# Five late projection chunks, output projection by input quarters, and the first gate through GpSimd's queue

## The chip, the cores and the metric

The kernel runs on one core of one Trainium2 chip. The metric is the device time of one execution in microseconds; the time before is the median of three runs. A profile of one further execution is read beside it. Five engines work side by side: TensorE (PE in the profile, PEld for its weight loads), VectorE (DVE), ScalarE (ACT), GpSimd (POOL) and SyncE (SP), which here only issues DMAs. Each engine runs its own instructions in order. DMAs are issued from the queues of SP, ACT and POOL, and a DMA that has to wait holds up what is behind it on its queue.

## The reference, cut to what matters

One encoder layer on x of 256 rows by 2048 columns, float32, with a conditioning vector c:

```python
mod = silu(c) @ mod_w + mod_b                  # 2048 x 12288
sh_m, sc_m, g_m, sh_f, sc_f, g_f = split(mod, 6)
h = x * (1 + sc_m) + sh_m
q, k, v = split(h @ w_qkv + b_qkv, [2048, 2560])   # 32 query heads, 8 key/value heads of 64
q, k = rope(q), rope(k)
o = softmax over keys with |q - k| <= 128, and a sink logit per head
y = o @ w_o + b_o                              # 2048 x 2048
x = layer_norm(2 ** 0.25 * x + (1 + g_m) * y)
h = x * (1 + sc_f) + sh_f
y = square(relu(h @ w1 + b1)) @ w2 + b2        # 2048 x 8192 x 2048
x = layer_norm(2 ** 0.25 * x + (1 + g_f) * y)
```

Every one of these weights is used once for 256 rows. Some 290 MB come from HBM in one execution.

## The kernel before, in words

**Products.** A float32 product is made of three matmuls in the rounded type float32r: each operand is split in a high and a low part, and `mm3` (L561) adds high x high (L562), high x low (L563) and low x high (L564) in PSUM.

**The weight stream.** All weights come as chunks of 1 MB (128 x 2048) in one written order, `S.q`, planned at L485 to L553. SP loads them into raw buffers (L236): eight at first (`raws` and `raws2`), five from attention step 1 on (`S.deep = False`). A projection chunk is made into two half chunks, each copied to its high part by ScalarE (`wh`, L281) and subtracted to its low part by VectorE (`wl`, L252); up to five halves of each stand ready. A modulation chunk is used straight from its raw buffer: a row chunk by TensorE (`Mod.step`, L336), a column chunk by VectorE (`Col.step`, L376, a multiply and reduce against the spread condition `cb`). `S.pump` advances the stream whenever a half chunk is done.

**Group by group.** The 2048 inputs of the first projection are taken in six groups of 128-wide k tiles (`MIXG`, 1, 1, 2, 4, 4, 4). Once the modulation of a group is there (`columns`, L405), `modulated(g)` makes h of that group: ScalarE the high part (L591), VectorE the full value and the low part (L592, L593). The chunk (g, c) is the part of the projection from group g to the output block c of 512 columns; block order `CORD` counts 4 = keys, 5 = values, 0 to 3 = queries. Each chunk is 24 matmuls of 128 x 512 and ends in `evict`, which adds the two PSUM banks to the accumulator in SBUF (L609), unless `CARRY` says that the next chunk of the same block goes on in the same banks. `ORDER` gives the chunks of each group that run before attention, and the modulation of group g + 1 is planned between the chunks of group g. `modulated(g + 1)` stands in the program in the middle of the last chunk of group g that `ORDER` names.

**Attention steps.** 16 steps of attention are interleaved with chunks that are left: step n takes one chunk. Each has `scores(n)` (L755, L762, exponentials L772), `normalise` (L784), the transposes of the step before (`probs_T`, L794, L796), and every second step `values` (L810, then L813 and L814, which split the result in high and low, `oT[j]`, one j for four steps). `LATE` lists the projection chunks that run in the first steps, `OUT_AT` is the step at which the output projection starts, and `SLOT_FILL` how many chunks of the remaining modulation (the first gate `m_gm` with 16, then that of the feed-forward) are planned in each step. Before, LATE has eight chunks and there are 24 steps, the last eight without scores.

**Output projection.** `project(p, c)` (L852) takes two quarters j of the attention's output at a time: two chunks into the same two PSUM banks, 48 matmuls, then VectorE evicts (p = 0: L890 into `ys` with the output bias; p = 1: L893 to L896, with the gate, the residual and the statistics). The last one, c = 3, keeps the rows apart: all matmuls of row tile 0, then of row tile 1, and `add_gated` (L816, L819 to L821) and the normalisation (`norm_scalars`, `normed`) directly behind each. `project_0(3)` (L899) applies the gate to what `ys` holds for c = 3 ahead of that.

**The first gate.** `m_gm.spread` (L450) transposes the gate to one row, writes that to DRAM (`rowm`, L458) and reads it back into all 128 partitions by two broadcasts (L460), all from ScalarE's queue, at the end of step 15. The buffers are two of the pool `gen` (`g4`).

**What sets the order.** The program is written out in the order above; a scheduler then orders each engine's instructions by what it takes for their readiness. The instructions of `modulated` are kept at their place in program order. Buffers come from pools: `gen` has 20 of 4 KB a partition, `gen2` (`g4b`) six, `psa` five PSUM banks.

Of the kernel before, what the change touches and what calls it, by code (L numbers as in the profile page):

```python
# [11 lines left out]
F32 = mybir.dt.float32  # L12
# [8 lines left out]
S = 256  # L21
NT = S // 128
NK = D // 128
# [5 lines left out]
LN_EPS = 1e-5  # L29
NEG = -1.0e30  # L30
BLK = 4
OUT_AT = 8
X_AT = 16
SLOT_FILL = (2, 1, 2, 1, 2, 1, 2, 1, 1, 2, 1, 2, 1, 2, 1, 2, 2, 2, 1, 2, 1, 2, 0, 0)
MIXG = (1, 1, 2, 4, 4, 4)
MIXP = (1, 1, 1, 2, 2, 2)
FFG = (4, 4, 4, 4)
# [34 lines left out]
def hybrid_kernel(ctx: ExitStack, tc: tile.TileContext, a, out: bass.AP):  # L72
    nc = tc.nc
    cst = ctx.enter_context(tc.tile_pool(name="cst", bufs=1))
    sml = ctx.enter_context(tc.tile_pool(name="sml", bufs=4))
# [238 lines left out]
    S = Stream()  # L314
# [4 lines left out]
    class Mod:  # L319
# [24 lines left out]
        def step(self, raw):  # L344
            w, kc, i = self.w, self.kc, self.i
            if i == 0:
                self.ps = psm.tile([128, 512], F32, name="pm")
            r = raw.rearrange("p (k j n) -> p k j n", k=kc // 2 if self.pairs else kc, j=4)
            self.i += 1
            last = self.i == self.n  # L350
            for k in range(kc):
                kt = i * kc + k
                if self.pairs:
                    if k % 2 == 0:
                        cols = [cact[:, kt + j // 2:kt + j // 2 + 1].to_broadcast([128, 32]) for j in range(4)]
# [67 lines left out]
    class Gate(Group):  # L423
# [26 lines left out]
        def spread(self, g):  # L450

            d, b = self.col[:, 8 * self.p:], self.gb[:, 8 * self.p:]
            nc.vector.tensor_tensor(d, d, b, op=OP.add)
            pt = pst.tile([128, 512], F32, name="pt")
            nc.tensor.matmul(pt[:NK, :128], self.col, ident, start=True, stop=True)
            r = sml.tile([NK, 128], F32, name="grow", bufs=1)
            nc.scalar.copy(r, pt[:NK, :128])
            nc.scalar.dma_start(self.row.rearrange("o (k n) -> (o k) n", k=NK), r)  # L458
            for h in range(2):
                nc.scalar.dma_start(g[h], self.row[:, h * 1024:h * 1024 + 1024].partition_broadcast(128))  # L460
            return lambda c: g[c // 2][:, (c % 2) * 512:(c % 2) * 512 + 512]

    def groups(which, sizes, prods, mb, dst):
# [11 lines left out]
    m_gf = Gate("f", 0, gateb[:, 1])  # L475

    G = len(MIXG)
    LATE = [(4, 3), (5, 3), (3, 4), (4, 4), (5, 4), (3, 5), (4, 5), (5, 5)]

    ORDER = {2: (1, 2, 0), 3: (0, 3, 2, 1), 4: (1, 2, 0), 5: (0, 1, 2)}  # L480
    CARRY = {((1, 2), 2), ((2, 0), 0), ((3, 1), 1), ((4, 0), 0)}
    CARRY |= {(x, x[1]) for x, y in zip(LATE, LATE[1:]) if x[1] == y[1]}
    qk_order = [(g, c) for g in range(2, G) for c in ORDER[g]]
    wq = lambda g, c: S.plan(a["wqkv"][m_mix[g].k0 * 6 // 4 + c])
# [10 lines left out]
    for g in range(2, G):  # L495
        n = len(ORDER[g])
        if g + 1 < G:
            S.side[len(S.q)] = lambda g=g: load_x(g)
        for x, c in enumerate(ORDER[g][1:], 1):
            if g + 1 < G:  # L500
                m_mix[g + 1].plan({2: [0, 0, 3], 3: [0, 3, 2, 2], 4: [0, 4, 4]}[g][x])
            wq(g, c)
        if g == 2:
            m_mix[3].plan(4)
        if g + 1 < G:
            if g == 3:
                m_mix[4].plan(1)
            wq(g + 1, ORDER[g + 1][0])
        if g == 2:
            m_mix[3].plan(1)  # L510
# [7 lines left out]
            if lp[0] < len(late):  # L518
                late[lp[0]].plan()

    OUTS = [(p, c, j) for p in range(2) for c in range(4) for j in (2 * p, 2 * p + 1)]
    for n in range(OUT_AT + 16):
        plan_late(SLOT_FILL[n])
        if n == X_AT:
            S.side[len(S.q)] = lambda: load_rows()
        if n < len(LATE):
            wq(*LATE[n])
        elif n >= OUT_AT and n - OUT_AT < len(OUTS):
            p, c, j = OUTS[n - OUT_AT]
            S.plan(a["wo"][c, j])  # L530
    S.stop = len(S.q)
    plan_late(4)
    W1_FILL = [1, 1, 1, 0, 0, 2, 0, 3, 0, 0, 0, 0, 0, 0, 0, 0]
# [27 lines left out]
    def mm3(ps, xh, xl, wh, wl, start, stop):  # L561
        nc.tensor.matmul(ps, xh, wh, start=start, stop=False)  # L562
        nc.tensor.matmul(ps, xh, wl, start=False, stop=False)  # L563
        S.prev = nc.tensor.matmul(ps, xl, wh, start=False, stop=stop).ins  # L564
# [284 lines left out]
        else:  # L849
            nc.vector.tensor_scalar(z, z, mv[:, 0:1], rstd, op0=OP.subtract, op1=OP.mult)  # L850

    def project(p, c):  # L852

        pss = [psa.tile([128, 512], F32, name="pa") for _ in range(NT)]
        last = p == 1 and c == 3
        ws = [S.main(), S.main()] if last else []
        for x in range(2):
            wh, wl = ws[x] if last else S.main()
            oh, ol = oT[2 * p + x]
            for r2 in (0, 2):  # L860
                for t in range(NT):
                    if last:
                        break
                    for r in (r2, r2 + 1):
                        s = slice(t * 512 + r * 128, t * 512 + r * 128 + 128)
                        mm3(pss[t], oh[:, s], ol[:, s], wh(r), wl(r), x + r == 0, x == 1 and r == 3)
                if not last:
                    S.done()
                    if r2 == 0 or x == 0:
                        yield  # L870
        if last:
            for t in range(NT):
                for x in range(2):
                    oh, ol = oT[2 * p + x]
                    wh, wl = ws[x]
                    for r in range(4):
                        s = slice(t * 512 + r * 128, t * 512 + r * 128 + 128)
                        mm3(pss[t], oh[:, s], ol[:, s], wh(r), wl(r), x + r == 0, x == 1 and r == 3)
                if t == 0:
                    yield  # L880
                add_gated(pss[t], t, c, g1, st)
                sc.append(norm_scalars(st[t]))
                normed(0, t)
            for _ in range(4):
                S.done(False)
            return
        for t, ps in enumerate(pss):
            y = part(ys, t, c)
            if p == 0:
                nc.vector.tensor_add(y, ps, bo(c))  # L890
            else:
                z = part(xs, t, c)
                nc.vector.tensor_add(y, y, ps)  # L893
                nc.vector.tensor_mul(y, y, g1(c))
                nc.vector.scalar_tensor_tensor(z, z, ALPHA, y, op0=OP.mult, op1=OP.add)
                nc.vector.bn_stats(st[t][:, c], z)  # L896
# [25 lines left out]
    S.behind = True  # L922
    for n in range(OUT_AT + 16):
        j, i = n // 4, n % 4
        if n < 16:
            scores(n)
        for f in todo:
            f()
        todo = []
        if n == 1:  # L930
            S.deep = False
        if n < OUT_AT:
            w = qkv(*LATE[n])
        else:
            if n == OUT_AT:
                assert all(h is raws for h in S.home[S.at:]), "an early buffer is still in use"
                ys, bo = [g4b() for _ in range(4)], bias_all(a["bo"], [g4b(), g4b()])
            if n % 2 == OUT_AT % 2:
                w = project(*divmod((n - OUT_AT) // 2, 4))
        mid = mids(n)  # L940
        if j < 3:
            if i == 2:
                turn = rope(j + 1, 1)
                mid += [lambda: next(turn), lambda: next(turn)]
            if i == 3:
                mid.append(lambda: qA.__setitem__(j + 1, next(turn)))
                mid.append(lambda: qT.__setitem__(j + 1, heads_T(qA[j + 1])))
        next(w, None)
        for f in mid:
            f()  # L950
        next(w, None)
        if 0 < n <= 16 and n % 2 == 0:
            todo.append(values(n - 1))
        if n == 15:
            g1 = m_gm.spread([g4(), g4()])
        if n == 16:
            warm = sml.tile([128, 1], F32, name="warm")
            nc.scalar.activation(warm, eps, AF.Sqrt)
            st = [sml.tile([128, 4, 6], F32, name=f"st{t}", bufs=2) for t in range(NT)]
        if n == 18:  # L960
            project_0(3)


# [291 lines left out]
```

## Time and profile before

| | before |
|---|---|
| median of three runs | 1125.22 us (1124.86 to 1127.91) |
| profiled execution | 1127.18 us |
| its span, first to last instruction | 1125.4 us |
| mean granted TensorE clock | 0.978 |
| busy: PE, DVE, ACT, POOL | 1067.9, 786.5, 526.9, 17.1 us |
| moved by DMA | 292.74 MB, 260 GB/s over the span |

The stages lie in the span as follows: groups 0 to 5 up to some 160 us, steps with scores from 163.69 us, the last output projection ends near 379 us, and the feed-forward part runs from 390 us to the end. In the rows, "[9.10 <-DVE g L814]" is the idle time of the engine before the instruction, and what ended it. PE busy is counted with modelled ends of its matmuls, so that one of 128 x 512 counts some 0.39 us, though the next starts after 0.23. A row of a stretch gives busy time and number of instructions for each engine, the granted clock, the DMA engines' busy share and GB/s.

### The profile page before, as it was taken

What the parts mean: (1) busy time and instruction counts of PE and PEld (TensorE: products, weight loads), DVE (VectorE), ACT (ScalarE), POOL (GpSimd) and SP (SyncE); (2) the same over time, 40 slices, a digit from 0 to 9 for tenths busy, and PEclk for the clock granted to TensorE, in tenths of its full rate; (3) what the DMA queues carried; (4) which work ended last, traced back from release to release, by engine and by line L of the source; (5) the groups of instructions that cost most, each with busy time, mean ns of one, the idle gap of its engine ahead of it and who ended that gap; (6) DMA issues with size and microseconds to landing.
All of it is one profiled execution on the core that took longest, in us unless ns stands there. A gap on an engine that the chain in (4) does not pass through costs nothing.

```text
span 1125.4 us, 16314 instructions
## 1 busy us (share of the span) xinstructions
PE 1067.9 (95%) x6554; PEld 883.0 (78%) x6554; DVE 786.5 (70%) x1135; ACT 526.9 (47%) x811; POOL 17.1 (2%) x34
## 2 busy tenths in 40 slices
PE   7687999999979899999999999999999999999995
PEld 6565777677757699998888888888888888888884
DVE  3786898778648966765668787865665656665576
ACT  5422447778643454653345444334444334444340
POOL 1000000000000000000000001000000000000001
PEclk9997999999998899999999999999999999999998
DMA  9999987777984888555678788776555555557521
GB/s 385 425 425 415 413 303 279 278 260 280 367 326 151 321 341 343 192 186 188 198 288 297 263 283 274 294 291 217 185 188 191 202 192 187 187 188 262 187 75 75
DMA packets 43651, 292.74 MB, mean 260 GB/s; under 512 B 4876, under 2 KB 5036, under 8 KB 9784
## 3 DMA queue, kind: packets, MB, share of 16 engines
q1 hardware_dynamic: 40400, 281.96, 67.5%
q0 software_dynamic: 1792, 6.29, 1.8%
q10 hardware_dynamic: 1384, 3.45, 0.8%
q8 instruction: 51, 0.84, 0.3%
q14 instruction: 24, 0.20, 0.0%
HBM read 289.57 MB, written 2.11 MB: 259 GB/s over the span
## 4 chain that ended last, share of the span: by engine, by line
PE 77%; DVE 9%; DMA 7%; ACT 4%; issue 2%; POOL 0%; DVEq 0%; ACTq 0%; POOLq 0%
PE pa L1081 16%; PE pa L564 14%; PE pa L562 14%; PE pa L563 14%; PE pa L1082 8%; DMA raw<-in_mod 5%; PE pa L1058 3%; PE pa L1059 3%; PE pa L1057 3%; DVE raw L376 2%; DVE wl L252 2%; PE pm L336 2%; DMA raw<-in_wqkv 1%; ACT wh L281 1%; ACT g L772 1%
## 5 line engine op out<-in xcount | busy, mean ns | idle before, releaser
L252 DVE TENSOR_TENSOR wl<-raw,wh 128x1024 fp32r<-128x1024 f32 x332 | 403.7, 1223 | 237.9 <-ACT wh L281 236.7
L281 ACT CAST wh<-raw 128x1024 fp32r<-128x1024 f32 x332 | 347.8, 1051 | 439.7 <-PE pa L564 258.7
L564 PE MATMUL pa<-wh,g 128*128 128x512 f32 x816 | 320.7, 394 | 14.0 <-DVE g L814 9.1
L562 PE MATMUL pa<-wh,g 128*128 128x512 f32 x816 | 325.2, 399 | 3.6 <-ACT g L591 2.2
L563 PE MATMUL pa<-wl,g 128*128 128x512 f32 x816 | 321.3, 394 | 0.0
L1081 PE MATMUL pa<-g,wh 128*128 128x512 f32 x768 | 271.6, 399 | 0.0
L1082 PE MATMUL pa<-g,wl 128*128 128x256 f32 x768 | 215.7, 281 | 0.0
L564 PEld LDWEIGHTS pa<-wh,g 128*128 128x128 f32 x816 | 154.6, 189 | 49.3 <-DVE g L814 10.0
L562 PEld LDWEIGHTS pa<-wh,g 128*128 128x128 f32 x816 | 154.9, 190 | 43.5 <-issue 7.1
L563 PEld LDWEIGHTS pa<-wl,g 128*128 128x128 f32 x816 | 155.0, 190 | 31.6 <-DVE wl L252 0.7
L1081 PEld LDWEIGHTS pa<-g,wh 128*128 128x128 f32 x768 | 144.3, 188 | 36.2 <-issue 0.2
L1082 PEld LDWEIGHTS pa<-g,wl 128*128 128x128 f32 x768 | 145.1, 189 | 0.1
L376 DVE CUSTOM_DVE_ANT_0 raw<-raw,cb 128x2048 f32<-128x2048 f32 x54 | 123.5, 2287 | 19.1 <-DMA raw<-in_mod 19.1
L1058 PE MATMUL pa<-g,wh 128*128 128x256 f32 x256 | 73.5, 288 | 2.0 <-DVE g L1001 2.0
L1057 PE MATMUL pa<-g,wh 128*128 128x256 f32 x256 | 73.2, 288 | 0.0
L1059 PE MATMUL pa<-g,wl 128*128 128x256 f32 x256 | 73.0, 286 | 0.0
L336 PE MATMUL pm<-raw,cact 128*32 128x128 f32 (+1 forms) x1216 | 46.6, 292 | 13.7 <-DMA raw<-in_mod 13.3
L336 PEld LDWEIGHTS pm<-raw,cact 128*32 128x32 f32 x1216 | 32.0, 111 | 28.1 <-DMA raw<-in_mod 14.5
L1058 PEld LDWEIGHTS pa<-g,wh 128*128 128x128 f32 x256 | 49.7, 194 | 2.8 <-DVE g L1001 2.3
L1057 PEld LDWEIGHTS pa<-g,wh 128*128 128x128 f32 x256 | 49.8, 195 | 0.4 <-ACT g L993 0.4
L1059 PEld LDWEIGHTS pa<-g,wl 128*128 128x128 f32 x256 | 49.8, 194 | 0.2 <-issue 0.2
L772 ACT ACTIVATE g<-g,nm 128x256 f32<-128x256 f32 x64 | 31.8, 498 | 23.4 <-DVE nm L762 23.3
(171 smaller groups left out, 673.8 us busy)
## 6 DMA issues: line engine op xcount, KB each, us to landing
raw<-in_mod SPq DMA_DIRECT2D x96, 1024.0 KB, 7.4
raw<-in_w SPq DMA_DIRECT2D x64, 1024.0 KB, 4.9
raw<-in_w1b SPq DMA_DIRECT2D x48, 1024.0 KB, 5.0
raw<-in_wqkv SPq DMA_DIRECT2D x24, 1024.0 KB, 10.7
raw<-in_wo SPq DMA_DIRECT2D x16, 1024.0 KB, 7.4
raw<-in_w1a SPq DMA_DIRECT2D x16, 1024.0 KB, 7.0
g<-in_x SPq DMA_DIRECT2D x4, 512.0 KB, 12.1
gb<-in_lnrow POOLq DMA_DIRECT2D x8, 256.0 KB, 6.1
```

What stands on the lines that cost most here:

```text
L252: self.pinned(nc.vector.tensor_sub(l, r, f32(self.hs[n])))
L281: self.pinned(nc.scalar.copy(h, s))
L336: i = nc.tensor.matmul(self.ps[32 * j:32 * j + 32, :w], lhsT[j] if type(lhsT) is list else lhsT, rhs[j], start=self.first, stop=stop)
L376: S.pinned(nc.vector.tensor_tensor_reduce(out=raw, in0=raw, in1=cb, scale=1.0, scalar=0.0, op0=OP.mult, op1=OP.add, accum_out=self.dst))
L562: nc.tensor.matmul(ps, xh, wh, start=start, stop=False)
L563: nc.tensor.matmul(ps, xh, wl, start=False, stop=False)
L564: S.prev = nc.tensor.matmul(ps, xl, wh, start=False, stop=stop).ins
L1057: nc.tensor.matmul(o, wh(w, 128), hh, start=new, stop=False)
L1058: nc.tensor.matmul(o, wh(w, 128), hl, start=False, stop=False)
L1059: nc.tensor.matmul(o, wl(w, 128), hh, start=False, stop=end)
L1081: nc.tensor.matmul(ps, wh(k, 128), hb, start=k == 0, stop=False)
L1082: nc.tensor.matmul(ps[:, :256], wl(k, 128), hb[:, :256], start=False, stop=k == NK - 1)
```

## The change

Three things, in one edit.

The chunks (3,5), (3,4) and (4,3) of the first projection leave `LATE` and are planned in `ORDER`, ahead of attention; the modulation chunks of the following groups are distributed anew between them. `LATE` has five chunks left, and there are 21 steps.

The output projection starts at step 5 instead of 8 and takes one quarter j at a time: first all four c of quarter 0, then of quarter 1, and so on; each `project` is one chunk with 24 matmuls and an eviction of its own. Quarter 0 brings the bias in, quarters 1 and 2 only add, quarter 3 adds, gates and takes the statistics. `SLOT_FILL` fills two modulation chunks into each of the first eight steps, so that the first gate's 16 chunks end with step 7's slot.

The first gate is spread at the end of step 12 instead of 15, by the same three DMAs on GpSimd's queue, into two buffers of `gen2`. `project_0(3)` follows at the end of step 16 instead of 18. The rows of x for the residual (`load_rows`) are loaded at stream position 79 instead of 89.

```diff
-OUT_AT = 8
-X_AT = 16
-SLOT_FILL = (2, 1, 2, 1, 2, 1, 2, 1, 1, 2, 1, 2, 1, 2, 1, 2, 2, 2, 1, 2, 1, 2, 0, 0)
+OUT_AT = 5
+X_AT = 10
+SLOT_FILL = (2, 2, 2, 2, 2, 2, 2, 2, 1, 1, 1, 1, 1, 2, 2, 2, 2, 2, 2, 1, 0)
...
-            nc.scalar.dma_start(self.row.rearrange("o (k n) -> (o k) n", k=NK), r)
+            nc.gpsimd.dma_start(self.row.rearrange("o (k n) -> (o k) n", k=NK), r)
             for h in range(2):
-                nc.scalar.dma_start(g[h], self.row[:, h * 1024:h * 1024 + 1024].partition_broadcast(128))
+                nc.gpsimd.dma_start(g[h], self.row[:, h * 1024:h * 1024 + 1024].partition_broadcast(128))
...
-    LATE = [(4, 3), (5, 3), (3, 4), (4, 4), (5, 4), (3, 5), (4, 5), (5, 5)]
-    ORDER = {2: (1, 2, 0), 3: (0, 3, 2, 1), 4: (1, 2, 0), 5: (0, 1, 2)}
-    CARRY = {((1, 2), 2), ((2, 0), 0), ((3, 1), 1), ((4, 0), 0)}
+    LATE = [(5, 3), (4, 4), (5, 4), (4, 5), (5, 5)]
+    ORDER = {2: (1, 0, 2), 3: (5, 4, 3, 0, 2, 1), 4: (1, 2, 3, 0), 5: (0, 1, 2)}
+    CARRY = {((1, 2), 2), ((2, 2), 5), ((3, 1), 1), ((4, 0), 0)}
...
-                m_mix[g + 1].plan({2: [0, 0, 3], 3: [0, 3, 2, 2], 4: [0, 4, 4]}[g][x])
+                m_mix[g + 1].plan({2: [0, 0, 3], 3: [0, 2, 2, 2, 1, 1], 4: [0, 3, 3, 2]}[g][x])
...
-            if g == 3:
-                m_mix[4].plan(1)
...
-    OUTS = [(p, c, j) for p in range(2) for c in range(4) for j in (2 * p, 2 * p + 1)]
+    OUTS = [(c, js, x) for js in ((0,), (1,), (2,), (3,)) for c in range(4) for x in range(len(js))]
...
-    def project(p, c):
+    def project(js, c):
...
+        for x in range(len(js)):
+            ws.append(S.main())
+            for r in (0, 2):
+                for t in range(NT):
+                    step(x, t, (r, r + 1))
+                S.done()
+                if r == 0 or x < end:
+                    yield
         for t, ps in enumerate(pss):
             y = part(ys, t, c)
-            if p == 0:
+            if n == 0:
                 nc.vector.tensor_add(y, ps, bo(c))
-            else:
+                continue
+            nc.vector.tensor_add(y, y, ps)
+            if n == 3:
                 z = part(xs, t, c)
-                nc.vector.tensor_add(y, y, ps)
                 nc.vector.tensor_mul(y, y, g1(c))
...
-            if n % 2 == OUT_AT % 2:
-                w = project(*divmod((n - OUT_AT) // 2, 4))
+            c, js, x = OUTS[n - OUT_AT]
+            if x == 0:
+                w = project(js, c)
...
-        if n == 15:
-            g1 = m_gm.spread([g4(), g4()])
+        if n == 12:
+            g1 = m_gm.spread([g4b(), g4b()])
+            st = [sml.tile([128, 4, 6], F32, name=f"st{t}", bufs=2) for t in range(NT)]
         if n == 16:
             warm = sml.tile([128, 1], F32, name="warm")
             nc.scalar.activation(warm, eps, AF.Sqrt)
-            st = [sml.tile([128, 4, 6], F32, name=f"st{t}", bufs=2) for t in range(NT)]
-        if n == 18:
             project_0(3)
```

More of the change, by code (lines that the diff above doesn't have):

```diff
@@ L527, in hybrid_kernel @@
             wq(*LATE[n])
-        elif n >= OUT_AT and n - OUT_AT < len(OUTS):
-            p, c, j = OUTS[n - OUT_AT]
-            S.plan(a["wo"][c, j])
+        else:
+            c, js, x = OUTS[n - OUT_AT]
+            S.plan(a["wo"][c, js[x]])
     S.stop = len(S.q)
@@ L850, in normed, with step @@
             nc.vector.tensor_scalar(z, z, mv[:, 0:1], rstd, op0=OP.subtract, op1=OP.mult)
-    def project(p, c):
+    def project(js, c):
         pss = [psa.tile([128, 512], F32, name="pa") for _ in range(NT)]
[L855 to L870, printed above, removed]
+        end, n = len(js) - 1, js[-1]
+        last = n == 3 and c == 3
+        ws = [S.main() for _ in js] if last else []
+        def step(x, t, rs):
+            wh, wl = ws[x]
+            oh, ol = oT[js[x]]
+            for r in rs:
+                s = slice(t * 512 + r * 128, t * 512 + r * 128 + 128)
+                mm3(pss[t], oh[:, s], ol[:, s], wh(r), wl(r), x + r == 0, x == end and r == 3)
         if last:
             for t in range(NT):
[L873 to L878, printed above, removed]
+                for x in range(len(js)):
+                    step(x, t, range(4))
                 if t == 0:
@@ L883, in project @@
                 normed(0, t)
-            for _ in range(4):
+            for _ in range(2 * len(js)):
                 S.done(False)
             return
+        for x in range(len(js)):
+            ws.append(S.main())
[5 more added lines that the diff above has]
+                    yield
         for t, ps in enumerate(pss):
             y = part(ys, t, c)
-            if p == 0:
+            if n == 0:
                 nc.vector.tensor_add(y, ps, bo(c))
-            else:
+                continue
+            nc.vector.tensor_add(y, y, ps)
+            if n == 3:
                 z = part(xs, t, c)
-                nc.vector.tensor_add(y, y, ps)
                 nc.vector.tensor_mul(y, y, g1(c))
@@ L937, in hybrid_kernel @@
                 ys, bo = [g4b() for _ in range(4)], bias_all(a["bo"], [g4b(), g4b()])
-            if n % 2 == OUT_AT % 2:
-                w = project(*divmod((n - OUT_AT) // 2, 4))
+            c, js, x = OUTS[n - OUT_AT]
+            if x == 0:
+                w = project(js, c)
         mid = mids(n)
```

## The prediction

> **What bounds the kernel now.** I began with the page: engine totals and the forty slices.
>
> ```profile
> span 1125.4 us, 16314 instructions
> PE 1067.9 (95%) x6554; PEld 883.0 (78%) x6554; DVE 786.5 (70%) x1135; ACT 526.9 (47%) x811; POOL 17.1 (2%) x34
> ...
> PE   7687999999979899999999999999999999999995
> ...
> PEclk9997999999998899999999999999999999999998
> DMA  9999987777984888555678788776555555557521
> ```
>
> TensorE is busy 95% of the span, and the change neither adds nor removes a matmul. So it can only gain where TensorE stands idle or runs at a lowered clock, and lose by making new such places. Two slices stick out below 400 us: the fourth (PEclk 7), while the DMA row is full, and the thirteenth and fourteenth (PEclk 8). The busy time by stretches and TensorE's waits name them:
>
> ```profile
> 78.00:100.00 22.00, 9.71 (x101) 6.72 (x94) 15.12 (x22) 3.28 (x6) 0.00 (x0) 0.61 1.01 427
> 100.00:320.00 220.00, 217.50 (x1507) 161.01 (x1506) 180.48 (x348) 142.22 (x319) 2.19 (x4) 1.00 0.83 315
> 340.00:346.00 6.00, 6.00 (x15) 4.71 (x16) 3.63 (x5) 1.04 (x1) 0.00 (x0) 0.51 0.16 22
> 392.00:1125.00 733.00, 720.48 (x3990) 621.52 (x3989) 487.74 (x600) 323.85 (x407) 9.86 (x14) 0.99 0.63 223
> ...
> PE pm L336 <- DMA raw<-in_mod: 13.3, 4, 6.5
> PE pa L564 <- DVE g L814: 9.1, 1, 9.1
> ```
>
> Columns are the stretch, its length, then PE, PEld, DVE, ACT and POOL busy, the granted clock, the DMA share and GB/s. From 100 to 320 us and from 392 us on TensorE is the bound: 217.50 of 220 and 720.48 of 733. What can be won lies at 78 to 100 us and around 330 us.
>
> **The gate's stall goes.** The timeline there:
>
> ```profile
> 321.03 0.32 ACTq L458 DMA_DIRECT2D rowm<-grow  x1
> 326.06 0.86 ACTq L460 DMA_DIRECT2D g<-rowm  x2
> 326.96 1.07 ACT L796 COPY g<-pt 128x512 f32<-128x512 f32 x2 [4.52 <-DMA rowm<-grow]
> 327.60 1.14 PE L810 MATMUL pa<-g,g 128*64 128x256 f32 x8 [0.87 <-ACT g L796]
> 337.40 0.69 DVE L903 TENSOR_TENSOR g4b<-g4b,g 128x512 f32<-128x512 f32 x1 [11.28 <-DMA g<-rowm]
> 339.14 0.69 DVE L814 TENSOR_TENSOR g<-pa,g 128x512 fp32r<-128x512 f32 x1
> 339.88 0.79 PE L564 MATMUL pa<-wh,g 128*128 128x512 f32 x1 [9.10 <-DVE g L814]
> ```
>
> ScalarE sends the gate row to DRAM at 321.03 and stands 4.52 us until it has landed, because the broadcast behind it on its queue reads it back. VectorE then stands 11.28 us at `project_0` (L903), which wants the broadcast, and a weight subtraction and the values' subtraction (L814) are queued behind it; TensorE wants those. Cost: 9.10 + 0.87 idle, and then 6 us (340 to 346) at a clock of 0.51, that is 6 x 0.49 = 3.0. Sum 13.0 us.
>
> [...]
>
> After, the spread is issued at the end of step 12 and first read at the end of step 16. Moved with it: VectorE's bias add, two matmuls, a ScalarE copy and three DMAs, all small. The three DMAs pass from ScalarE's queue to GpSimd's, which has nothing behind them but the second bias's load, not wanted before the feed-forward outputs. GpSimd's own wait is for one DMA, and nobody else queues there. The pitch of a step:
>
> ```profile
> 163.69 1.14 PE L755 MATMUL pa<-g,g 64*128 64x256 f32 x8
> 308.76 0.92 PE L755 MATMUL pa<-g,g 64*128 64x256 f32 x6
> ...
> g4b<-in_bo POOLq DMA_DIRECT2D x2, 512.0 KB, 4.5
> ...
> 180.00:200.00 20.00, 19.32 (x131) 13.56 (x128) 18.08 (x39) 13.48 (x35) 1.23 (x2) 1.00 0.66 233
> ```
>
> Scores of steps 0 and 15 lie 145.1 us apart: 9.67 us a step, so the lead is 4 x 9.67 = 38.7 us against 337.40 - 321.03 = 16.4 for row and broadcast as they are. Slack 22.3. A GpSimd-queue broadcast of the same size takes 4.5 us to land, in a stretch where VectorE is busy 18.08 of 20. Term: -13.0 (0 if the cover failed). The new buffers `g4b` are the output bias's, last read in step 8; no wait.
>
> **The third group may start sooner.** TensorE ends group 2 just before 77.57 us and starts group 3 at 90 to 95.65:
>
> ```profile
> 74.90 0.16 DVE L421 TENSOR_TENSOR modm<-pt,pack 128x4 f32<-128x4 f32 x1 [1.34 <-PE pt L419]
> 77.57 1.08 PE L336 MATMUL pm<-raw,cact 128*32 128x128 f32 x32
> 80.02 1.08 PE L336 MATMUL pm<-raw,cact 128*32 128x128 f32 x32 [1.37 <-DMA raw<-in_mod]
> 81.98 2.29 DVE L376 CUSTOM_DVE_ANT_0 raw<-raw,cb 128x2048 f32<-128x2048 f32 x1
> 87.55 1.94 PE L336 MATMUL pm<-raw,cact 128*32 128x128 f32 x32 [6.45 <-DMA raw<-in_mod]
> 89.77 2.07 ACT L591 ACTIVATE g<-g,modm 128x256 fp32r<-128x256 f32 x4
> 92.51 2.29 DVE L376 CUSTOM_DVE_ANT_0 raw<-raw,cb 128x2048 f32<-128x2048 f32 x1 [1.90 <-DMA raw<-in_mod]
> 94.72 0.41 DVE L592 TENSOR_SCALAR g<-g,modm 128x256 f32<-128x256 f32 x1
> 95.17 0.43 DVE L593 TENSOR_TENSOR g<-g,g 128x256 fp32r<-128x256 f32 x1
> 95.65 0.79 PE L564 MATMUL pa<-wh,g 128*128 128x512 f32 x1 [4.00 <-DVE g L593]
> ```
>
> Group 3's own modulation was complete at 75 us; its activation (L591, 89.77) and subtraction (L593) run only behind group 4's modulation weights: the last row chunk (TensorE, 87.55) and the last column chunk (VectorE, 92.51), both waiting for DMA. Numbering the weight stream from 0, these are chunks 31 and 33. In program order the modulation follows chunk 28 (the row at 80.02); after the change it follows chunk 27 (the column at 81.98), and group 4's last row and column move to 32 and 34. Which order the scheduler now writes I can't read off the trace. Best: the subtraction follows the column at 81.98: 81.98 + 2.29 + 0.41 + 0.43 = 85.1 instead of 95.17 + 0.43 = 95.6, -10.5. Worst: it still follows the last column, one 1 MB chunk later at 427 GB/s, +2.5. I take -7, nearer the best, because the program now reaches it before chunk 28 and two more projection chunks lie between it and group 4's last row.
>
> The three chunks that come forward, (3,5), (3,4), (4,3), bring 3 x 2.5 = 7.4 us of DMA into the full stretch, but 3 x 5.46 = 16.4 us of matmuls too (24 a chunk, 0.227 us apart: below, six in 1.36), so groups 4 and 5 arrive behind more work than before. Term 0; 7.4 if that cover were gone.
>
> **What is added.** An output projection by quarters leaves PSUM four times, not two.
>
> ```profile
> 349.62 0.39 PE L564 MATMUL pa<-wh,g 128*128 128x512 f32 x1
> 350.98 0.39 PE L564 MATMUL pa<-wh,g 128*128 128x512 f32 x1
> ...
> L890 DVE TENSOR_TENSOR g4b<-pa,g4b x8: 662/688/692, 258.9 to 318.6; 128x512 f32<-128x512 f32 x8
> ...
> L562 PEld LDWEIGHTS pa<-wh,g 128*128 128x128 f32 x121 | 22.7, 188 | 9.4 <-issue 4.7 <-DVE g4b L890 0.7 <-DVE g L609 0.3
> ```
>
> Out: 14 adds become 30. Projection: 38 become 44, as (3,4), (3,5) and (4,3) no longer hand their banks on. 22 adds x 0.69 = 15 us of VectorE, spread over 270 us in which it has 20% free (180.48 of 220). On the path: in 160 to 310 us TensorE's weight loads waited 0.7 us for L890 in three evictions, 0.23 each; 8 more evictions cost 1.9, I take 2 (0 to 5). The eight gate columns now fall in steps 0 to 4 and before, where VectorE was busy 18.08 of 20: 1 (0 to 5). The four row loads of `x` on SP's queue move some five steps forward; about two steps of weights stand loaded ahead of them (five buffers), and 2 MB at 427 GB/s are 4.9 us: 0, or 4.9 if nothing covered them.
>
> **The tail.** Steps 17 to 23 become 17 to 20.
>
> ```profile
> 367.97 1.28 DVE L893 TENSOR_TENSOR g4b<-g4b,pa 128x512 f32<-128x512 f32 x2
> 373.90 2.29 DVE L376 CUSTOM_DVE_ANT_0 raw<-raw,cb 128x2048 f32<-128x2048 f32 x1
> 376.11 0.69 DVE L819 TENSOR_TENSOR tmp<-pa,g 128x512 f32<-128x512 f32 x1
> 379.29 0.69 DVE L819 TENSOR_TENSOR tmp<-pa,g 128x512 f32<-128x512 f32 x1 [0.55 <-PE pa L564]
> ```
>
> After the last but one column's matmuls VectorE takes 376.11 - 367.97 = 8.1 us until the first half's gating (L819), 3.2 more to the second's. Before, 48 matmuls (10.9 us) ran meanwhile, and the second L819 waited for TensorE. After, 24 run (5.46 us), so it comes 11.3 - 5.9 = 5 us behind TensorE; without the column chunk in between some 2. I take +3 (1.7 to 5).
>
> **Sum.** -13 - 7 + 2 + 1 + 3 = -14. The profiled execution took 1127.18 us (1125.4 span, 1.8 around it), so 1113.2; it lies 2.0 above the median of the runs, 1125.22, so I predict 1111.2, say 1111. Best: -13 - 10.5 + 1.7 = -22, 1103. What a measurement can tell from no change is 0.3%, 3.4 us.
>
> **Rivals.**
>
> Group 3 stays behind the whole of group 4: +2.5 in place of -7, sum -4.5, 1120.7. For it: the order was so in the trace, though the program put chunk 28 last. Against: the program's point moved up.
>
> [...]
>
> Slower: the banks. Every step now takes two fresh PSUM banks of five and must evict them before the next step's projection. If each eviction stood behind a column chunk, 2.3 + 1.3 us less the 1.1 of scores between, 2.5 us a step in the 12 steps 5 to 16 would be 30: -13 - 7 + 30 + 1 + 3 = +14, 1139. It decides from -13 - 7 + 1 + 3 + 12w = +3.4, w = 1.6 us a step. Against it stand the 0.23 us that an eviction cost in the trace.
>
> **Numbers.** Forecast 0.60 (nearly all faster), group 3 behind 0.21 (two thirds of it faster), late gate 0.07 (mostly same), banks or a new stall of that size 0.12 (slower). So faster 0.75, same 0.13, slower 0.12. The likeliest case alone spans 1103 to 1118; the range 1102 to 1124 takes in the next two.
>
> **What would show it.** The 9.10 us wait for L814 and VectorE's 11.28 at `project_0` are gone, and the clock is 1.00 all through the attention steps: the gate. The first group-3 matmul lies at 84 to 90 us, with L591 ahead of group 4's last row: the early part. Evictions to `g4b` without TensorE gaps: the banks. The feed-forward stretch keeps its 733 us. I am wrong if a wait on a row of `in_mod` beyond 6 us stays before group 3, if TensorE idles at each step, or if the last normalisation starts over 5 us after the last projection.

## The result and the profile after

The changed kernel took 1121.55 us (median of 7 runs, 1116.23 to 1123.08), the kernel before 1126.6 beside it: ratio 0.9943, 95% interval 0.9922 to 0.9965. It is faster, by about 5 us between the medians (6.4 between the means of the same runs) and not by the 14 forecast. The 1121.55 us lie inside the stated range, next to the 1120.7 given for group 3 staying behind; as the profile shows, group 3 did not stay behind, so that nearness is chance. The same instruction streams ran a second time as `pin_sqrt` below: 0.9933 (0.9920 to 0.9945). Where several runs are compared, ratios to the kernel before stand, times 1127 us: the change brought 6.4 to 7.6 us.

The profiled execution took 1123.08 us, the longest of the seven. Its page, engine totals and slices:

```profile
span 1121.3 us, 16337 instructions
...
PE 1071.7 (96%) x6554; PEld 884.6 (79%) x6554; DVE 799.9 (71%) x1157; ACT 526.8 (47%) x811; POOL 20.3 (2%) x40
...
PEclk9999999998999799999999999999999999999998
```

The dips of before in slices 4 and 13 are gone from the clock row; slice 14 is deeper (7, before 8), and slice 10 is new. Busy time by stretches (stretch, length, PE, PEld, DVE, ACT, POOL, clock, DMA share, GB/s):

```profile
78.00:100.00 22.00, 20.89 (x172) 16.07 (x171) 17.74 (x25) 4.87 (x7) 0.00 (x0) 1.00 1.01 426
100.00:320.00 220.00, 211.45 (x1460) 155.45 (x1462) 187.51 (x349) 133.86 (x295) 2.81 (x5) 0.98 0.84 322
370.00:392.00 22.00, 11.37 (x110) 9.15 (x113) 17.92 (x44) 12.84 (x20) 0.00 (x0) 0.69 0.87 344
392.00:1121.00 729.00, 716.16 (x3954) 617.47 (x3942) 483.80 (x593) 321.08 (x403) 11.49 (x17) 0.99 0.63 221
```

From 78 to 100 us TensorE is busy 20.89 of 22 instead of 9.71. From 100 to 320 it stood idle 8.55 instead of 2.5, and between the last projection and the feed-forward half of its time. The three places in the timeline, first group 3 and the gate:

```profile
76.07 2.08 ACT L589 ACTIVATE g<-g,modm 128x256 fp32r<-128x256 f32 x4 [0.42 <-DVE modm L421]
80.87 0.43 DVE L591 TENSOR_TENSOR g<-g,g 128x256 fp32r<-128x256 f32 x1
81.35 0.50 PE L562 MATMUL pa<-wh,g 128*128 128x512 f32 x1 [1.11 <-DVE g L591]
...
307.33 0.50 POOL L458 DMA_DIRECT2D rowm<-grow  x1 [105.89 <-ACT grow L457]
311.23 1.08 POOL L460 DMA_DIRECT2D g4b<-rowm  x2 [3.40 <-DMA rowm<-grow]
...
342.69 0.69 DVE L901 TENSOR_TENSOR g4b<-g4b 128x512 f32<-128x512 f32 x1
```

Group 3's activation (now L589) stands at 76.07 instead of 89.77, and TensorE takes its first matmul at 81.35. The gate's broadcast is issued at 311.23 and first read at 342.69, with no wait (the landing took 10.0 us). Both gains are there. Then the attention steps (L753 scores, L717 and L722 rotation, L738 and L739 transposing its result):

```profile
170.24 1.72 PE L753 MATMUL pa<-g,g 64*128 64x256 f32 x8 [0.24 <-ACT g L739]
...
238.69 1.13 PE L753 MATMUL pa<-g,g 64*128 64x256 f32 x8
241.62 0.68 DVE L717 TENSOR_TENSOR g<-g,trig 128x512 f32<-128x512 f32 x1
246.54 1.21 DVE L722 TENSOR_TENSOR g<-g,g 128x1024 f32<-128x1024 f32 x1
249.65 1.14 PE L738 MATMUL pt<-ident,g 128*128 128x128 f32 x8 [0.25 <-ACT g L794]
252.53 1.05 ACT L739 COPY g<-pt 128x512 f32<-128x512 f32 x2
253.16 1.23 PE L753 MATMUL pa<-g,g 64*128 64x256 f32 x4 [2.37 <-ACT g L739]
255.76 0.63 PE L561 MATMUL pa<-wl,g 128*128 128x512 f32 x1
...
325.98 1.13 PE L753 MATMUL pa<-g,g 64*128 64x256 f32 x8
```

Scores of steps 0 and 15 lie 155.7 us apart, and 152.8 in the profile of `pin_sqrt`, which has the same streams; before, 145.1. Two more modulation row chunks done in between account for 2.1 of the difference. The rotation and step 7's scores before:

```profile
227.15 1.28 DVE L719 TENSOR_TENSOR g<-g,trig 128x512 f32<-128x512 f32 x2
230.40 1.13 PE L755 MATMUL pa<-g,g 64*128 64x256 f32 x8
```

In the kernel before the rotation (L719) began ahead of step 7's scores (230.40), and steps 6 to 8 took 31.1 us. In step 7 of the changed kernel VectorE begins the rotation for step 8 only behind step 7's scores, at 241.62. The sum follows at 246.54, the transposes at 249.65, ScalarE's copies at 252.53, and step 8's scores wait 2.37 us for them. TensorE then runs at a lower clock (0.50 from 255 to 259 us, 0.63 us a matmul instead of 0.39). Steps 7 and 8 took 26.9 us; steps 6 to 8, the fairer measure because half of step 6's values went into step 7, took 35.5. VectorE had not been too full for an earlier rotation: from 227.9 to 238.9 us it stood idle five times, 3.7 us in all, without taking it; in VectorE's order the rotation stood behind the first masking of step 7's scores (L760, 240.00 to 241.62). Last, the first normalisation:

```profile
369.70 1.28 DVE L817 TENSOR_TENSOR tmp<-pa,g4b 128x512 f32<-128x512 f32 x2
373.76 0.15 DVE L825 TENSOR_SCALAR ve<-mv 128x1 f32<-128x1 f32 x1
374.83 1.04 ACT L281 CAST wh<-raw 128x1024 fp32r<-128x1024 f32 x1 [9.76 <-DMA raw<-in_w1a]
375.89 1.28 ACT L827 ACT_TABLE_LOAD   x1
377.19 0.29 ACT L827 ACTIVATE sd<-ve 128x1 f32<-128x1 f32 x2
378.15 2.29 DVE L376 CUSTOM_DVE_ANT_0 raw<-raw,cb 128x2048 f32<-128x2048 f32 x1
380.36 0.54 DVE L848 TENSOR_SCALAR g<-g,mv,r 128x512 f32<-128x512 f32 x1
380.96 0.69 PE L985 MATMUL pt<-ident,g 128*128 128x128 f32 x2 [8.45 <-DVE g L848]
384.26 1.01 PE L1055 MATMUL pa<-g,wh 128*128 128x256 f32 x3 [0.32 <-ACT g L991]
```

The variance is ready at 373.9, but ahead of the square root ScalarE's queue holds a cast of feed-forward weights that waits 9.76 us for its load, and the table load behind it. Then a column chunk (L376) stands ahead of the first normalised tile (L848). TensorE idles 8.45 us. Before, table load and square roots stood ahead of the cast:

```profile
366.76 1.28 ACT L829 ACT_TABLE_LOAD   x1
378.77 0.20 ACT L829 ACTIVATE sd<-ve 128x1 f32<-128x1 f32 x1 [10.73 <-DVE ve L827]
382.17 1.99 ACT L281 CAST wh<-raw 128x1024 fp32r<-128x1024 f32 x2
```

The load was late as well: SP issued it at 367.14, after standing up to 14.4 us for raw buffers with modulation row chunks that TensorE had not yet used, and from 360 to 365 us the DMA share was 0.01 (before, as far ahead of the last projection's end, 0.81 from 365 to 370 us and 0.51 from 370 to 375).

### The profile page after: what moved, and what is told of

Read it like the earlier page. It is cut to its first block, busy times and chain, and to the rows that moved or that the text cites. A ratio compares the mean times of both kernels' runs of the same rounds, so it can differ in the third digit from the quotient of the medians.

```text
span 1121.3 us, 16337 instructions
## 1 busy us (share of the span) xinstructions
PE 1071.7 (96%) x6554; PEld 884.6 (79%) x6554; DVE 799.9 (71%) x1157; ACT 526.8 (47%) x811; POOL 20.3 (2%) x40
## 4 chain that ended last, share of the span: by engine, by line
PE 83%; DVE 8%; DMA 4%; issue 3%; ACT 2%; SPq 0%; POOL 0%; DVEq 0%; POOLq 0%; ACTq 0%
PE pa L1079 16%; PE pa L560 15%; PE pa L561 14%; PE pa L562 14%; PE pa L1080 8%; PE pa L1056 3%; PE pa L1057 3%; PE pa L1055 3%; DMA raw<-in_mod 3%; PE pm L336 3%; DVE raw L376 2%; DVE wl L252 2%; PE pa L753 1%; ACT wh L281 1%; PE pt L792 1%
## 5 line engine op out<-in xcount | busy, mean ns | idle before, releaser
L561 PEld LDWEIGHTS pa<-wl,g 128*128 128x128 f32 x816 | 154.7, 190 | 35.5 <-DVE wl L252 3.3
L1080 PEld LDWEIGHTS pa<-g,wl 128*128 128x128 f32 x768 | 145.1, 189 | 0.1
L376 DVE CUSTOM_DVE_ANT_0 raw<-raw,cb 128x2048 f32<-128x2048 f32 x54 | 123.4, 2286 | 19.8 <-DMA raw<-in_mod 19.8
```

The costliest lines, as they stand in the source:

```text
L376: S.pinned(nc.vector.tensor_tensor_reduce(out=raw, in0=raw, in1=cb, scale=1.0, scalar=0.0, op0=OP.mult, op1=OP.add, accum_out=self.dst))
L1080: nc.tensor.matmul(ps[:, :256], wl(k, 128), hb[:, :256], start=False, stop=k == NK - 1)
```

## The experiments

**The parts in turn.** The gate alone, on the kernel before:

```
-            nc.scalar.dma_start(...)          # row and both halves of the broadcast
+            nc.gpsimd.dma_start(...)
-        if n == 15:
+        if n == 12:
             g1 = m_gm.spread([g4(), g4()])
```

> The kernel before with the first gate spread at the end of step 12 on GpSimd's queue, and nothing else (its buffers stay in gen). Theory: the gate's stall is worth its 13 us by itself, so 12 to 13 us less than before, with neither the 9.1 us wait for L814 nor the cold stretch behind it; this one kernel would then be faster than the whole change. Rival: only the other parts of the change made the gain, and the stall's room is taken by another wait: within 4 us of before.

Measured: 1114.22 us, ratio 0.9890 (0.9876 to 0.9903), so -12.4 us. It beats the whole change. The next run adds the quarters, with eight late chunks and the projection from step 8 as before (`project_0(3)` then follows at step 19):

```
-    OUTS = [(p, c, j) for p in range(2) for c in range(4) for j in (2 * p, 2 * p + 1)]
+    OUTS = [(c, js, x) for js in ((0,), (1,), (2,), (3,)) for c in range(4) for x in range(len(js))]
```

> The kernel before (eight late chunks, output projection from step 8) with the gate early on GpSimd's queue and the output projection by quarters. Theory: against the gate alone the evictions by quarters and the shorter last chunk cost: 4 to 8 us slower than the gate alone, with the loss in the first normalisation and little in steps 0 to 7. Rival: quarters are free and the loss in the attention steps is that of the earlier modulation chunks: within 2 us of the gate alone.

Measured: 1119.24 us, ratio 0.9936 (0.9922 to 0.9950): the quarters cost 5.2 us. To part tail from evictions, quarters for two inputs and a pair for the last two:

```
-    ... for js in ((0,), (1,), (2,), (3,)) ...
+    ... for js in ((0,), (1,), (2, 3)) ...
```

> The gate spread early and the projection from the eighth step, with quarters for the first two inputs alone and the last two inputs paired as before, so the last chunk again has 48 matmuls and there are 6 fewer adds than with four quarters. The gate alone took 1114.2 us, with four quarters 1119.2. Theory A, the tail: the 5 us are lost because the last chunk's first half no longer has 24 matmuls of the second half over it; then nearly all comes back: 1114 to 1116. Theory B, evictions: the adds and banks cost it; then about two fifths at most comes back: 1117 to 1119.5.

Measured: 1115.2 us, ratio 0.9896 (0.9882 to 0.9911). 4.5 of the 5.2 us come back, as theory A said: it is the tail. The pair saves four of the 16 evictions too, but what is left against the gate alone, with eight, is only 0.7 us, inside the intervals. With the pair the first half's gating stands at 363.89, while TensorE still multiplies the second half until 366.9; with quarters both halves' gating (L819 x2) came together at 368.48, behind a column chunk. There the square roots still stood ahead of the cast (372.56 and 376.16), so the order on ScalarE that the changed kernel shows is a further loss.

**Which part of the gate.** Lead and queue were changed together. One run moves the step and keeps ScalarE's queue, the other moves the queue and keeps step 15.

> The kernel before with the gate spread moved from step 15 to step 12 alone; its DMAs stay on ScalarE's queue. On GpSimd's queue at step 12 the time was 1114.2 us. Theory: the lead is what counts; ScalarE's wait of some 4.5 us for the row is covered by TensorE's work: 1113 to 1117. Rival: the wait on ScalarE comes back at TensorE, as the copy of the transposed probabilities stands behind it: 1117 to 1121.

> The kernel before with the spread's three DMAs on GpSimd's queue alone, at step 15 as before. Theory: row and broadcast take some 15 us on either queue, so the stall at the first multiplication by the gate stays nearly whole, only ScalarE's 4.5 us of waiting go: 1123 to 1127. Rival: the queue is what cost, then it falls to 1114 to 1118.

Measured: the earlier step alone 1114.89 us, ratio 0.9892 (0.9878 to 0.9905); the queue alone 1126.13 us, ratio 0.9991 (0.9983 to 1.0000). The timelines, first of the queue alone, then of the step alone:

```profile
338.25 0.69 DVE L903 TENSOR_TENSOR g4b<-g4b,g 128x512 f32<-128x512 f32 x1 [9.30 <-DMA g<-rowm]
339.60 0.79 PE L564 MATMUL pa<-wh,g 128*128 128x512 f32 x1 [9.08 <-DVE g L814]
```

```profile
290.78 0.38 ACTq L458 DMA_DIRECT2D rowm<-grow  x1
297.13 0.51 ACT L772 ACTIVATE g<-g,nm 128x256 f32<-128x256 f32 x1 [6.38 <-DMA rowm<-grow]
```

On GpSimd's queue at step 15 the stall stays (9.08 us). On ScalarE's queue at step 12 ScalarE stands 6.38 us, and TensorE covers it. All of the gain that these runs can tell is the lead.

**Group 3 alone.** The gate alone, with the modulation one chunk sooner:

```
-        if g < G - 1 and at == len(ORDER[g]) - 1:
+        if g < G - 1 and at == len(ORDER[g]) - (2 if g == 2 else 1):
             mid.append(lambda: modulated(g + 1))
```

> The gate alone, with the modulation of input group 3 emitted one projection chunk sooner, at chunk (2,2) in place of (2,0); eight late chunks and pairs stay. Theory: waiting behind group 4's modulation weights cost time of its own; then scores start 5 to 10 us sooner and the whole takes 1105 to 1110 against 1114.2. Rival: up to the first scores the weight stream is the bound (DMA share 0.95 to 0.99 before 163 us), so an earlier group 3 only waits later; then scores start under 3 us sooner and it takes 1111.5 to 1115. In the second case what the changed kernel won there came from the three chunks that moved in, not from the order.

Measured: 1106.4 us, ratio 0.9820 (0.9805 to 0.9835), so 7.9 us on top of the gate (5.7 between the two profiled spans). The activation (here L591) now stands before group 4's weights:

```profile
72.31 2.08 ACT L591 ACTIVATE g<-g,modm 128x256 fp32r<-128x256 f32 x4 [1.96 <-DVE modm L421]
```

The first scores start at 159.72 instead of 164.43, and the lead is kept to the end. These two edits bring 20.3 us; against them the changed kernel is 12.7 to 13.9 us slower. That is a net figure: its first scores start 10.5 us later than here (170.24), though 16.4 us of matmuls (three chunks) were moved ahead of them, so by this reckoning some 6 us of that work found room, and more than the net figure is lost behind it.

**The evictions.** The changed kernel without 16 of its additions:

```
             if n == 0:
                 nc.vector.tensor_add(y, ps, bo(c))
                 continue
-            nc.vector.tensor_add(y, y, ps)
             if n == 3:
+                nc.vector.tensor_add(y, y, ps)
```

> The changed kernel without the 16 additions of quarters 1 and 2 (those quarters' products are left out of the output; all matmuls stay). If the evictions by quarters hold up the attention steps, scores 0 to 15 come down from 155.7 us by 5 us or more and the time by as much. If they are hidden, as the 0.23 us an eviction in the trace of before said, it is 0 to 2 us.

Measured: 1120.64 us, ratio 0.9947 (0.9935 to 0.9960), no gain. But the run says little, for without the additions the first multiplication by the gate came 22 us sooner in VectorE's order, ahead of its rows:

```profile
320.22 1.29 DVE L901 TENSOR_TENSOR g4b<-g4b 128x512 f32<-128x512 f32 x2 [11.16 <-DMA g4b<-rowm]
327.93 1.98 PE L808 MATMUL pa<-g,g 128*64 128x256 f32 x8 [6.90 <-ACT g L794]
```

The same was tried later on the kernel with both mends (below):

> The kernel with both mends (thinner slots, normalisation first), without the 16 additions of the second and third input's projections to the sum; their products are computed and don't reach the output. With the additions it took 1107.8 us. Theory: 16 x 0.69 = 11 us of VectorE hidden under TensorE, so under 2 us come back: 1105.5 to 1108. Rival: the evictions hold the banks or VectorE at the steps' ends, then 4 us or more come back: 1104 or less. If the gate's rows are late again for the first multiplication, the trace shows it as a wait of VectorE on the broadcast, and that is to be taken off first.

Measured: 1114.91 us, ratio 0.9888 (0.9871 to 0.9905), slower than the 1107.76 with the additions, and the gate's wait was there again (VectorE 10.89 us, TensorE 6.63, and a clock of 0.68 from 320 to 328 us). Off that place the additions can be priced: from the scores of step 0 to those of step 13 it took 128.0 us against 129.0, from step 15's to the last projection 42.0 against 43.2. So they cost about 2.2 us, read from one profile of each kernel; two profiles of the same streams (the changed kernel and `pin_sqrt`) differ by 2.9 us from step 0 to step 15, so this shows that the cost is small and not its size. What a kernel without them and without the stall would take was not measured.

**The square root.** An attempt to hold it in its place in program order:

> The changed kernel with the two square roots of the first normalisation held at their place in program order on ScalarE. Theory: the root waits there behind the first feed-forward chunk's copy, which waits for its DMA; held ahead of it, the root comes 3.4 us sooner and the time falls by 3 to 5 us. Rival: the normalisation is set by VectorE, whose subtraction and column chunk stand ahead anyway: under 1 us.

Measured: 1118.71 us, ratio 0.9933 (0.9920 to 0.9945). The edit left ScalarE's order as it was (cast, table load at 372.24, square root at 373.53), so it told nothing of the cast; it is a second reading of the changed kernel. The next one did move it:

```
+                if "cast" in self.hold:
+                    tc.add_manual_dep(i.ins, self.hold["cast"].name, ORDER_ONLY, reason="hold")
...
+            if "col" in S.hold:
+                tc.add_manual_dep(i.ins, S.hold["col"].name, ORDER_ONLY, reason="hold")
...
+        S.hold["cast"] = nc.scalar.activation(sd, ve, AF.Sqrt).ins
...
-    S.vecs(4)
+    S.vecs(2)
...
     h2 = [ff_input(0)]
+    S.vecs(2)
```

> The whole change, with the first normalisation put ahead of other work on its two engines: the casts of the feed-forward weights are ordered behind both square roots on ScalarE, and the two modulation column chunks that stood between the last projection and the first normalised tile on VectorE are ordered behind the first feed-forward input. The changed kernel took 1121.6 us, and 1118.7 when its instruction streams ran a second time. Theory: from the last projection matmul (370.20) to the first feed-forward matmul (384.26) it lost 10.6 us of TensorE because the square root stood behind a cast that waited for its load (some 3.4 us) and 2.3 us behind a column chunk, so this order gives 4 to 6 us back: 1113 to 1117. Rival: the weights' loads are what comes last (the cast waited 9.76 us for one), then the order gives under 1.5 us: 1117 to 1121.

Measured: 1113.96 us, ratio 0.9888 (0.9871 to 0.9904): 5.1 to 6.2 us back.

```profile
361.40 1.28 ACT L834 ACT_TABLE_LOAD   x1
365.41 0.69 DVE L824 TENSOR_TENSOR tmp<-pa,g4b 128x512 f32<-128x512 f32 x1 [1.04 <-PE pa L569]
369.44 0.20 ACT L834 ACTIVATE sd<-ve 128x1 f32<-128x1 f32 x1 [6.76 <-DVE ve L832]
370.82 0.54 DVE L855 TENSOR_SCALAR g<-g,mv,r 128x512 f32<-128x512 f32 x1
371.11 1.99 ACT L282 CAST wh<-raw 128x1024 fp32r<-128x1024 f32 x2 [1.04 <-DMA raw<-in_w1a]
371.42 0.44 PE L992 MATMUL pt<-ident,g 128*128 128x128 f32 x2 [2.93 <-DVE g L855]
```

The table load is done at 362.7 while ScalarE waits anyway, the first half's gating starts while TensorE still works on the second, and the casts still wait for their load (until 371.11), but only after the square roots. From the last projection to the first feed-forward matmul it now takes 9.2 us instead of 14.1; before the change it was 8.5, so the order takes back most of what was lost there. The edit moves ScalarE's casts and VectorE's column chunks together, and the run doesn't part the two.

**The attention steps.** Other slots, with the same chunks in the same order:

```
-SLOT_FILL = (2, 2, 2, 2, 2, 2, 2, 2, 1, 1, 1, 1, 1, 2, 2, 2, 2, 2, 2, 1, 0)
+SLOT_FILL = (2, 1, 1, 2, 2, 1, 1, 2, 2, 1, 2, 2, 2, 2, 2, 2, 2, 2, 2, 1, 0)
```

> The whole change with the modulation chunks of the attention steps spread otherwise: 2,1,1,2,2,1,1,2,2,1,2 in place of two in each of the first eight steps, and two a step from the twelfth on; the sum and the order stay. The changed kernel took 1121.6 us, and 1118.7 on a second run. Theory: steps 0 to 15 took 155.7 us against 145.1 because the rotations and the gate columns together fill VectorE (10.00 busy of 10 us at 160, 200 and 280), so thinner slots in front of them give back 2 to 4 us: 1115 to 1119. Rival: the work is the same and comes later: within 1 us of 1119 to 1121.

Measured: 1111.44 us, ratio 0.9858 (0.9845 to 0.9872): 8.5 to 9.6 us back, over twice what the theory allowed. In this kernel:

```profile
168.49 2.08 PE L753 MATMUL pa<-g,g 64*128 64x256 f32 x8
233.41 1.29 DVE L717 TENSOR_TENSOR g<-g,trig 128x512 f32<-128x512 f32 x2
236.26 1.14 PE L753 MATMUL pa<-g,g 64*128 64x256 f32 x8
246.21 1.13 PE L753 MATMUL pa<-g,g 64*128 64x256 f32 x8
316.84 1.13 PE L753 MATMUL pa<-g,g 64*128 64x256 f32 x8
```

The rotation (L717) comes before step 7's scores (236.26) and step 8's (246.21) wait for nothing: steps 7 and 8 take 20.6 us (6 to 8: 32.0), and the scores of steps 0 and 15 lie 148.4 apart. VectorE's busy time is not smaller (80.4 us from 160 to 250 us, in the changed kernel 77.6). So it may be the order and not the load. The next run changes only the order, with the changed kernel's own slots:

```
-            if i == 2:
+            if i == 1:
                 turn = rope(j + 1, 1)
```

> The whole change with its own slots, and each rotation of the next head group begun one step sooner, at the second step of a group of four in place of the third; the same work. In the changed kernel TensorE waited 2.37 us for the transposed heads before the scores of step 8 and then ran at a clock of 0.66 from 250 to 260 us, because VectorE came to the rotation (241.62) only behind step 7's scores; steps 7 and 8 took 26.9 us, with thinner slots 20.6. Theory: what is lost in the attention steps hangs on when the rotation comes, not on the sum of VectorE's work; then the scores of steps 0 and 15 lie 147 to 151 us apart in place of 152.8 to 155.7 and the time is 1112 to 1117. Rival: VectorE has too much to do in steps 0 to 8 whatever the order; then another wait takes the place and the time stays at 1118 to 1122.

Measured: 1116.07 us, ratio 0.9900 (0.9887 to 0.9914): 3.7 to 4.8 us back, scores 149.7 apart (170.67 to 320.34), as the theory said. So about half of what the slots gave is the rotation's lateness, shown by itself. The rest of their effect (first scores at 168.49 instead of 170.24, less work before step 4) was not taken apart.

**Together.**

> The whole change with both mends, the thinner slots (1111.4 us alone) and the first normalisation ahead of the casts and column chunks (1114.0 alone, 4.8 to 7.6 under the changed kernel). Theory: they lie in different places, steps 0 to 9 and after 360 us, and add: 1104 to 1107. Rival: the columns put off in the one are what the other put off too, and they collide behind the normalisation: 1108 to 1111.

> The kernel with both mends and the rotation begun one step sooner. Theory: thinner slots had already brought the rotation in time (step 8's scores wait for nothing there), so it gives under 1.5 us: 1106 to 1108.5. Rival: the two are separate losses and add: 1103 to 1105.

Measured: slots and normalisation together 1107.76 us, ratio 0.9821 (0.9805 to 0.9837); with the earlier rotation too 1105.47 us, ratio 0.9805 (0.9792 to 0.9819). Slots and normalisation give back 12.6 to 13.8 us, less than their sum (13.6 to 15.8). The rotation adds 1.8, within the two intervals: the median lies between the two ranges expected, so whether it adds anything is not settled. This is the fastest kernel run here, but its interval overlaps that of the gate and the earlier group 3 alone (0.9805 to 0.9835). Five late chunks and quarters, once mended, brought nothing beyond those two edits that these runs can tell. The mends were not tried on that kernel.

## Why the prediction missed, step by step

**Gate, -13.0.** Right: -12.4. The 9.10 and the 11.28 us are gone. The change of queue did not matter; the lead did all (0.9890 and 0.9892 at step 12 on the two queues, 0.9991 with the queue alone). The late gate, to which I gave 0.07, did not come in this change. That row and broadcast take longer than the lead of 38.7 us was not shown: on GpSimd's queue their median landings add up to 13.3 us in the changed kernel (3.3 and 10.0) and 16.7 in the gate alone (5.3 and 11.4). What both kernels without the additions show is another way to the same wait (11.16 and 10.89 us on VectorE): the 22 us of slack that I worked out held for one order of VectorE's work only.

**Group 3, -7.** The mechanism was right, the size partly luck. The activation runs ahead of group 4's rows, and the first rival is out. But the first dependent matmul came at 81.35 (I had said 84 to 90), 14.3 us sooner than before and beyond my best case of 10.5, while the sum passed such a lead on whole. It is not: with the earlier group 3 alone TensorE has less than full work from 100 to 120 us (8.86 and 7.07 us busy of 10 each), and the first scores start only 4.7 us sooner. The time fell by 7.9 (5.7 between the profiled spans).

**Evictions, +2.** Nothing speaks against it: some 2.2 for the 16 additions, read from single profiles, and 0.7 between eight and twelve evictions. The rival of the banks is out as I put it; TensorE does idle in the steps, but for transposed heads (2.37 us before step 8's scores).

**Gate columns on VectorE, +1 (0 to 5).** This step failed. I priced the columns by VectorE's free share (18.08 of 20 busy) and put a whole-engine average in place of the question what is queued behind them. The thinner slots gave back 8.5 to 9.6 us, beyond the 5 of my range. With two chunks in each early step VectorE came to the rotation a step later, and four stages hang on it in line (rotation, transposes, copies, scores); an earlier rotation by itself gave back 3.7 to 4.8. It was the written order that came late, not the columns' own time: only one column chunk stood in the 19 us ahead of the rotation, and VectorE idled there. What makes up the other half of the slots' effect stays open. I had a row of 1.00 clock and 217.50 of 220 busy for these steps and took it as given that they stay so.

**Tail, +3 (1.7 to 5).** The mechanism that I priced is there: the shorter last chunk costs 4.5 us (quarters against a pair), inside the range. What failed is that the sum had no term for a second one. I counted VectorE's column chunks; I had not followed ScalarE's queue, where in the changed kernel the cast with its load came ahead of the table load and the square root. Ordering the casts and the column chunks behind gave back 5.1 to 6.2 us. My own sign of being wrong, the last normalisation over 5 us behind the last projection, came true: square root at 377.19, last matmul at 369.81.

**The sum.** The gains were forecast at -20 and measured at -20.3 (with luck in group 3's share). The losses were forecast at +6; net they were 12.7 to 13.9, and other slots with another order of the first normalisation gave back about as much (12.6 to 13.8).

## What to carry to other kernels

When work moves into a stretch where the bounding engine is 99% busy (217.50 of 220 us here, before), ask which chain of small steps on the other engines ends at it (here rotation, transpose, copy, scores), and where that chain will stand in each engine's written order once the work is added; a free share of 10% (18.08 of 20 us busy here) said nothing of that. Near a stage's end follow every engine's queue: here a cast that waited 9.76 us for its load stood in front of the square root that the critical chain wanted next. And run the parts of a change one by one: the earlier gate and, by a smaller edit, the earlier group 3 were worth 20 us, the whole 6 to 8.

## What the runs showed of the hardware

After a gap of 2.37 us on TensorE its clock was lower in some executions and not in others. Before step 8's scores the gap is the same in three profiles (2.36 or 2.37 us). In the changed kernel matmuls then started 0.43 us apart from 255.76 to 259.18 us, and 0.24 from 259.51. From 250 to 260 us the clock was 0.66 in the changed kernel, 0.83 in `pin_sqrt` with the same streams, and 1.00 in `ln_first` (shown in this order):

```profile
250.00:260.00 10.00, 7.63 (x28) 5.46 (x27) 6.15 (x16) 6.27 (x18) 0.00 (x0) 0.66 0.57 203
250.00:260.00 10.00, 7.71 (x34) 6.12 (x35) 6.20 (x15) 7.40 (x21) 0.00 (x0) 0.83 0.53 194
250.00:260.00 10.00, 7.64 (x45) 6.09 (x44) 7.15 (x18) 8.23 (x22) 0.00 (x0) 1.00 0.59 207
```

Steps 6 to 8 took 35.5, 34.2 and 32.6 us in these three, before 31.1 with one modulation row chunk (1.1 us) more: without any lowered clock the three steps lost 1.5 us and that chunk's, and with it up to 2.9 more. The lowered clock was 0.50 in the changed kernel (255 to 259 us). Taking that for both profiles, I estimate from the means of 0.66 and 0.83 over 10 us that it lasted 6.8 and 3.4 us (0.34 and 0.17 of 10 us, over 0.50).

The gate's broadcast, two DMAs of 512 KB, took about as long on either queue (11.4 and 9.9 us at step 12, median from issue to landing):

```profile
g<-rowm POOLq DMA_DIRECT2D x2, 512.0 KB, 11.4
```

```profile
g<-rowm ACTq DMA_DIRECT2D x2, 512.0 KB, 9.9
```

The first is the gate alone at step 12 on GpSimd's queue, the second the same step on ScalarE's. At step 15 it is the other way round: 7.5 on GpSimd's queue, 9.2 on ScalarE's, so the difference does not keep its sign; and in the changed kernel it was 10.0. I had taken 4.5 us for it from the output bias, a transfer of the same size.
